# A delta-rule recurrence that takes keys times state from the values before one product with the inverse

## The chip, the cores and the metric

The kernel runs on one core of one Trainium2 chip. The metric is the device time of one execution in microseconds (us), as the median of several runs; a profile is taken of one further execution. The core's engines run side by side: TensorE (PE; its weight loads are shown apart as PEld), VectorE (DVE), ScalarE (ACT), GpSimd (POOL) and SyncE (SP), which issues most transfers. Each engine works through its own instructions in a fixed order, and waits on semaphores for the others.

## The reference, cut to what matters

One inference step of a two-layer hybrid encoder over 1024 prompt frames (with 16 meta tokens ahead) and 32 sample frames. Layer 0 holds eight gated-delta heads beside an S5 state-space unit; their outputs go through one output projection. Layer 1 is attention; each layer ends in a SwiGLU block. The part that concerns us is the recurrence of a delta head over chunks, in fp32:

```python
    rhs = jnp.concatenate([vc * bc[..., None], kc * (bc * jnp.exp(gc))[..., None]], axis=-1)
    sol = lax.linalg.triangular_solve(a_low + jnp.eye(CHUNK, dtype=a_low.dtype), rhs,
                                      left_side=True, lower=True)
    u, w = sol[..., :dv], sol[..., dv:]
    qk = jnp.where(causal, jnp.einsum('nbhid,nbhjd->nbhij', qc, kc) * decay, 0.0)

    def step(S, blk):
        q_, k_, u_, w_, qk_, g_ = blk
        v_new = u_ - jnp.einsum('bhcd,bhde->bhce', w_, S)
        o = (jnp.einsum('bhcd,bhde->bhce', q_ * jnp.exp(g_)[..., None], S)
             + jnp.einsum('bhij,bhje->bhie', qk_, v_new))
        g_last = g_[..., -1:]
        S = (S * jnp.exp(g_last)[..., None]
             + jnp.einsum('bhcd,bhce->bhde', k_ * jnp.exp(g_last - g_)[..., None], v_new))
        return S, o
```

With Z the inverse of the triangular matrix, u is Z times the scaled values and w is Z times the scaled keys, so that v_new = Z (values) - (Z keys) S = Z (values - keys S). The state S is a 128x128 matrix per head.

## The kernel before

Everything lies with features in partitions and tokens along the free axis. A head's tokens are cut into nine chunks: chunk 0 holds the 32 sample tokens and, from partition 64 on, the 16 meta tokens; chunks 1 to 8 hold 128 prompt tokens each. Earlier stages have written to DRAM, for each head, the keys, values and queries (`qkvd`), the transposed inverse of each chunk (`invd`, loaded as `ZT`) and the decayed scores (`qkd`). `egt` holds the decays exp(g), one column per chunk and head.

`recur(h)` (from L1148) runs for the eight heads. **Preparation:** SP loads k, v, ZT, the scores and the queries. In three blocks of four, four and one chunk, TensorE transposes the keys (L1165) and the values (L1172) into the PSUM tile `bg` (two buffers); ScalarE scales the keys by the decay into `ke` (L1168, one instruction per chunk); VectorE makes `kd` (L1169) and the scaled values `vk` (L1174). Then TensorE multiplies ke with the inverse (L1179), and ScalarE copies that, negated, to `nw` (L1180), so nw is -w. kd, vk and nw are slots of the tile `bw` (six buffers).

**The chunk loop** (from L1192), in one PSUM bank of `rca` for even heads and `rcb` for odd ones: inverse times values (L1195) plus nw times the state S (L1199; L1197 in chunk 0, with the sample state) make the new values, which VectorE copies out as `vn` (L1201). TensorE multiplies kd with vn (L1213; L1205 and L1209 in chunk 0), VectorE makes the new state `Sa` or `Sb` (L1214; L1206, L1211). Scores times vn (L1216) and queries times the old state (L1220; L1218) make the output, copied by ScalarE (L1221, L1223). **Head end:** norms, a GpSimd scaling of all outputs (L1232), nine transposes (L1237), the product with the gate and a store to `mixd`.

Two other kinds of work stand between these steps on TensorE. The S5 unit's gated product (`s5.glu`) multiplies gh and gl with gwh and gwl: 144 products, lines L72 to L74 into `pm`. The output projection (`out_part`) does the same with rh, rl and wh, wl; its first part reads S5's output back from `mixd` into `rraw` (L1258), one of four tiles at a time, which ScalarE and VectorE split (L37, L38); 168 of its products stand in one stretch, between steps of heads 3 and 4, 60 after the last head. They are called fillers below. An fp32 product of 128 columns is two MATMUL records in the trace; the fillers are one each.

What sets the order: the kernel is written head after head, and `tile.TileContext` with `schedule_with_timeline_sim=True` (L2057) orders each engine's instructions ahead of the run, by the planner's own model of times, by dependences and by free buffers. On the chip the order of an engine is fixed.

Of the kernel before, what the change touches and what calls it, by code (L numbers as in the profile page):

```python
# [773 lines left out]
def even_layer(cx, ctx, I, O):  # L774
# [13 lines left out]
    with ExitStack() as es:  # L788
# [34 lines left out]
        with ExitStack() as esA:  # L823
# [98 lines left out]
            v.tensor_copy(stats.rearrange("p c q -> p (c q)"), pt[:, :360])  # L922
            egt = pool.tile([128, 9, 8], F32, name="egt")
            sc.activation(egt, stats[:, :, 32:40], AF.Exp)


            sm_all = pool.tile([128, 8, 8, 9], F32, name="gsm")
# [220 lines left out]
        def recur(h):  # L1148
            sm, egl = smalls[h]
            nk, nq, rk, rq, Pm, kds = (sm[:, i] for i in (0, 1, 2, 3, 4, 6))  # L1150
            P = "ab"[h % 2]
            k, vv = bslot("bk", 2), bslot("bk", 2)
            ZT, qk, qe = (bslot("bl", 6) for i in range(3))
            nc.sync.dma_start(k[:, :TG], qkvd[8 + h])
            nc.sync.dma_start(vv[:, :TG], qkvd[16 + h])
            nc.sync.dma_start(ZT, invd[h])
            nc.sync.dma_start(qk, qkd[h])
            nc.sync.dma_start(qe[:, :TG], qkvd[h])
            Zv, qv = c3(ZT), c3(qk)
            ke = bslot("ke", 1)  # L1160
            kd, vk = bslot("bw", 6), bslot("bw", 6)
            for a, b in BK:
                p = gpt()
                for c in range(a, b):
                    nc.tensor.transpose(p[:, (c - a) * 128:(c - a + 1) * 128], k[:, C0[c]:C0[c] + 128], cx.ident)  # L1165
                pv = p[:, :(b - a) * 128].rearrange("p (c i) -> p c i", i=128)
                for c in range(a, b):
                    sc.activation(c3(ke)[:, c], pv[:, c - a], AF.Copy, scale=egt[:, c, h:h + 1])  # L1168
                v.tensor_mul(c3(kd)[:, a:b], pv, kds[:, a:b].unsqueeze(2).to_broadcast([128, b - a, 128]))  # L1169
                p = gpt()  # L1170
                for c in range(a, b):
                    nc.tensor.transpose(p[:, (c - a) * 128:(c - a + 1) * 128], vv[:, C0[c]:C0[c] + 128], cx.ident)  # L1172
                pv = p[:, :(b - a) * 128].rearrange("p (c i) -> p c i", i=128)
                v.tensor_mul(c3(vk)[:, a:b], pv, nk[:, a:b].unsqueeze(2).to_broadcast([128, b - a, 128]))  # L1174
            nw = bslot("bw", 6)
            for a, b in BK:
                p = gpt()
                for c in range(a, b):
                    nc.tensor.matmul(p[:, (c - a) * 128:(c - a + 1) * 128], c3(ke)[:, c], Zv[:, c], start=True, stop=True)  # L1179
                sc.activation(c3(nw)[:, a:b].rearrange("p c i -> p (c i)"), p[:, :(b - a) * 128], AF.Copy, scale=-1.0)  # L1180
            g.memset(c3(nw)[:, 0, 32:128], 0.0)
            q0 = bp.tile([128, 128], F32, name="q0" + P)
            g.memset(q0[:, 32:], 0.0)
            g.tensor_copy(q0[:, :32], qe[:, :32])

            o = vk
            ov = c3(o)
            ss = bp.tile([128, 9], F32, name="oss" + P)
            S = None
            Ss = bp.tile([128, 128], F32, name="Ss", bufs=2)  # L1190
            nc.sync.dma_start(Ss, I['sdelta'][h])
            for c in range(9):  # L1192
                bank = rct(P)
                p = bank[:, 0:128]
                nc.tensor.matmul(p, Zv[:, c], c3(vk)[:, c], start=True, stop=False)  # L1195
                if c == 0:
                    nc.tensor.matmul(p, c3(nw)[:, 0], Ss, start=False, stop=True)  # L1197
                else:
                    nc.tensor.matmul(p, c3(nw)[:, c], S, start=False, stop=True)  # L1199
                vn = bp.tile([128, 128], F32, name="vn" + P, bufs=2)  # L1200
                v.tensor_scalar_mul(vn, p, Pm[:, c:c + 1])  # L1201
                p2 = bank[:, 128:256]
                Sn = bp.tile([128, 128], F32, name="S" + P, bufs=3)
                if c == 0:
                    nc.tensor.matmul(p2, c3(kd)[0:32, 0], vn[0:32], start=True, stop=True)  # L1205
                    v.scalar_tensor_tensor(Sn, Ss, egl[:, 9:10], p2, op0=OP.mult, op1=OP.add)  # L1206
                    g.dma_start(O['delta'][1, h], Sn)
                    p2 = bank[:, 384:512]
                    nc.tensor.matmul(p2, c3(kd)[64:80, 0], vn[64:80], start=True, stop=True)  # L1209
                    Sn = bp.tile([128, 128], F32, name="S" + P, bufs=3)  # L1210
                    v.tensor_copy(Sn, p2)  # L1211
                else:
                    nc.tensor.matmul(p2, c3(kd)[:, c], vn, start=True, stop=True)  # L1213
                    v.scalar_tensor_tensor(Sn, S, egl[:, c:c + 1], p2, op0=OP.mult, op1=OP.add)  # L1214
                p3 = bank[:, 256:384]
                nc.tensor.matmul(p3, qv[:, c], vn, start=True, stop=False)  # L1216
                if c == 0:
                    nc.tensor.matmul(p3, q0, Ss, start=False, stop=True)  # L1218
                else:
                    nc.tensor.matmul(p3, qe[:, C0[c]:C0[c] + 128], S, start=False, stop=True)  # L1220
                sc.activation(ov[:, c], p3, AF.Copy)  # L1221
                jk = bp.tile([128, 128], F32, name="jk" + P)
                sc.activation(jk, ov[:, c], AF.Square, accum_out=ss[:, c:c + 1])  # L1223
                S = Sn
            g.dma_start(O['delta'][0, h], S)
            t = sm[:, 7]
            v.tensor_mul(t, rq, rq)
            v.tensor_mul(t, t, ss)
            sc.activation(t, t, AF.Sqrt, scale=1.0 / (128.0 * 128.0), bias=cx.eps)
            v.reciprocal(t, t)  # L1230
            v.scalar_tensor_tensor(t, t, 128.0 ** -0.5, rq, op0=OP.mult, op1=OP.mult)
            g.tensor_mul(ov, ov, t.unsqueeze(2).to_broadcast([128, 9, 128]))  # L1232
            mx = bslot("mx", 1)
            for a, b in BK:
                p = rct(P)
                for c in range(a, b):
                    nc.tensor.transpose(p[:, (c - a) * 128:(c - a + 1) * 128], ov[:, c], cx.ident)  # L1237
                if a == 0:
                    rg = ((0, 32, 0), (64, 80, 32), (128, 512, 48))
                else:  # L1240
                    rg = ((0, (b - a) * 128, a * 128 - 80),)
                for x0, x1, t0 in rg:
                    n = x1 - x0
                    sc.activation(mx[:, t0:t0 + n], p[:, x0:x1], AF.Copy, scale=og[:, 0:1])
            z = xp.tile([128, T], F32, name="zr")
            nc.sync.dma_start(z, zd[h])
            g.tensor_mul(mx[:, :T], mx[:, :T], z)
            sc.dma_start(mixd[h], mx[:, :T])
# [826 lines left out]
```

## Time and profile before

| | us |
|---|---|
| median of three runs | 3353.06 |
| lowest and highest | 3349.21, 3353.29 |
| profiled execution | 3346.38 |
| its span | 3344.6 |

The profile is of the one profiled execution; its times count from the start of the span. 1.8 us of that execution lie outside the span. The mean granted TensorE clock was 0.971 of full speed. A group of a view names line, engine, operation, output and input tile; "idle before" is the time that the engine stood still just ahead of an instruction, and the arrow names what ended it. The stage around the change runs from 708 to 937 us.

### The profile page before, as it was taken

The page shows a single profiled execution, that of the slowest core. Times are in us where ns is not written, and L with a number is a line of the kernel's source. Part 1 is how long each engine was busy: PE and PEld are TensorE (multiplying, and loading weights), DVE is VectorE, ACT ScalarE, POOL GpSimd, SP SyncE. Part 2 cuts the span into 40 slices and gives each one's busy share as a digit, 9 for nine tenths or more (in the row PEclk, how much of TensorE's full clock was granted, in tenths as well). Part 3 has the DMA queues.
Part 4 walks back from the last instruction along what each step waited for, and adds up shares of the span by engine and source line. Part 5 has one row for each costly group of instructions (what it writes and reads, how often), then busy time and mean ns, then how long its engine had stood idle before and what let it go on. Part 6 is the DMA issues. An engine that isn't in the chain of part 4 may idle for free. (4 is left out here: it accounts for less than half of the span.)

```text
span 3344.6 us, 54676 instructions
## 1 busy us (share of the span) xinstructions
PE 3171.3 (95%) x21673; PEld 3042.8 (91%) x21673; DVE 1925.0 (58%) x3654; ACT 1190.3 (36%) x2219; POOL 1004.1 (30%) x1021
## 2 busy tenths in 40 slices
PE   7998999989999999999999999988998999999997
PEld 6998998888989999999999998876888999999996
DVE  8666548945437655556346226656767655556434
ACT  5543222135434322223123115555655322223112
POOL 2144664522200555540003002222210555551003
PEclk9999999999999999999999999997998999999998
DMA  3354323356432222226123455544415222226211
GB/s 111 130 170 156 119 89 108 93 187 253 156 128 78 83 78 78 78 85 229 49 60 131 150 142 143 158 143 123 134 66 182 79 80 80 78 77 217 74 46 67
DMA packets 159785, 391.87 MB, mean 117 GB/s; under 512 B 41037, under 2 KB 70497, under 8 KB 159529
## 3 DMA queue, kind: packets, MB, share of 16 engines
q1 hardware_dynamic: 134920, 319.49, 30.1%
q10 hardware_dynamic: 16704, 44.33, 3.6%
q0 software_dynamic: 7904, 24.56, 2.2%
q8 instruction: 171, 2.80, 0.3%
q14 instruction: 86, 0.70, 0.1%
HBM read 267.09 MB, written 121.20 MB: 116 GB/s over the span
## 5 line engine op out<-in xcount | busy, mean ns | idle before, releaser
L72 PE MATMUL pm<-mv,wh 128*128 128x352 f32 (+2 forms) x2272 | 750.6, 331 | 20.1 <-DVE pre L940 9.0
L74 PE MATMUL pm<-mv,wl 128*128 128x352 f32 (+2 forms) x2272 | 747.6, 330 | 0.5 <-DVE wl L38 0.5
L73 PE MATMUL pm<-mv,wh 128*128 128x352 f32 (+2 forms) x2272 | 747.5, 329 | 0.0
L72 PEld LDWEIGHTS pm<-mv,wh 128*128 128x128 f32 (+1 forms) x2272 | 428.8, 189 | 30.8 <-issue 8.6
L73 PEld LDWEIGHTS pm<-mv,wh 128*128 128x128 f32 (+1 forms) x2272 | 428.4, 189 | 3.9 <-issue 0.9
L74 PEld LDWEIGHTS pm<-mv,wl 128*128 128x128 f32 (+1 forms) x2272 | 428.5, 189 | 3.7 <-DVE wl L38 0.8
L37 ACT ACTIVATE wh<-wraw 128x512 fp32r<-128x512 f32 (+4 forms) x182 | 148.8, 818 | 664.0 <-PE pm L73 560.8
L255 PE MATMUL pq<-mv,wl 128*128 128x268 f32 x2112 | 294.5, 290 | 9.1 <-DVE xslot L265 4.2
L255 PE MATMUL pq<-mv,wh 128*128 128x268 f32 x2112 | 288.9, 287 | 3.7 <-DVE xslot L262 1.9
L255 PEld LDWEIGHTS pq<-mv,wl 128*128 128x128 f32 x2112 | 277.5, 192 | 9.8 <-ACT mv L37 4.4
L255 PEld LDWEIGHTS pq<-mv,wh 128*128 128x128 f32 x2112 | 272.2, 188 | 4.6 <-ACT wh L37 4.5
L104 POOL TENSOR_TENSOR acc<-acc,sq 128x360 f32<-128x360 f32 (+3 forms) x35 | 35.5, 1014 | 512.1 <-ACT sq L103 511.6
L342 DVE TENSOR_TENSOR xslot<-xslot,pm 128x360 f32<-128x360 f32 x144 | 74.8, 525 | 168.3 <-PE pm L74 168.2
L236 POOL TENSOR_TENSOR sab<-wraw 128x512 f32<-128x512 f32 x20 | 26.0, 1300 | 459.8 <-DMA wraw<-in_w_dram 373.3
L38 DVE TENSOR_TENSOR wl<-wraw,wh 128x512 fp32r<-128x512 f32 (+4 forms) x144 | 134.6, 935 | 47.2 <-ACT wh L37 45.7
L947 DVE SCALAR_TENSOR_TENSOR cy<-pre,convw,cy 128x1104 f32<-128x1104 f32 x72 | 114.0, 1583 | 16.1 <-ACT cy L945 15.2
L309 POOL TENSOR_TENSOR xslot<-xslot,r 128x1072 f32<-128x1072 f32 x44 | 120.9, 2770 | 0.1
L255 PE MATMUL pq<-us,wl 128*128 128x268 f32 x858 | 119.2, 287 | 0.0
L255 PE MATMUL pq<-us,wh 128*128 128x268 f32 x858 | 118.6, 286 | 0.0
L38 DVE TENSOR_TENSOR wh<-sab,wh 128x512 fp32r<-128x512 f32 x88 | 75.6, 861 | 68.1 <-ACT wh L37 68.1
L255 PEld LDWEIGHTS pq<-us,wl 128*128 128x128 f32 x858 | 111.6, 189 | 0.0
L255 PEld LDWEIGHTS pq<-us,wh 128*128 128x128 f32 x858 | 111.0, 188 | 0.0
(773 smaller groups left out, 7062.8 us busy)
## 6 DMA issues: line engine op xcount, KB each, us to landing
ud<-xslot SPq DMA_DIRECT2D x44, 536.0 KB
sab<-ud SPq DMA_DIRECT2D x44, 536.0 KB
wraw<-in_w_dram SPq DMA_DIRECT2D x44, 512.0 KB
xraw<-in_w_dram SPq DMA_DIRECT2D x44, 512.0 KB
wraw<-in_wie_dram SPq DMA_DIRECT2D x36, 512.0 KB
qkvd<-cy ACTq DMA_DIRECT2D x24, 552.0 KB
wraw<-in_wio_dram SPq DMA_DIRECT2D x24, 512.0 KB
kq<-qkvd SPq DMA_DIRECT2D x16, 552.0 KB
```

The lines of the kernel that those rows point to most:

```text
L37: nc.scalar.activation(h, src, AF.Copy)
L38: (eng or nc.vector).tensor_sub(l, src, f(h))
L72: nc.tensor.matmul(ps, a, h[:, c0:c1], start=start and k == 0, stop=False)
L73: nc.tensor.matmul(ps, a, l[:, c0:c1], start=False, stop=False)
L74: nc.tensor.matmul(ps, b, h[:, c0:c1], start=False, stop=stop and k == kt - 1)
L104: (eng or nc.gpsimd).tensor_add(acc[:, c0:c1], acc[:, c0:c1], s)
L236: eng.tensor_add(S1, A21, A22)
L255: nc.tensor.matmul(p[:, 512 * j:512 * j + HC], op[:, wo + 128 * k:wo + 128 * k + 128], B[nm][k][:, xo + HC * j:xo + HC * j + HC], start=ne ...
L309: g.tensor_mul(o, o, r)
L342: nc.vector.tensor_add(X[m][:, c0:c1], X[m][:, c0:c1], p)
L947: v.scalar_tensor_tensor(y[:, :TG], pre[:, j:j + TG], convw[:, i, j:j + 1], y[:, :TG], op0=OP.mult, op1=OP.add)
```

## The change

The product of keys and inverse, its scaling and its copy are taken out. In each chunk, the untransposed keys are multiplied with the state (L1188 of the new kernel), VectorE multiplies that with the decay, now negated once on GpSimd, and adds the values (`u`, L1189, in the place of vk); one product with the inverse (L1191) and the copy L1193 give vn. From there on it is as before under new numbers: L1197 to L1206 make the state, L1208, L1210 and L1212 the output, L1229 transposes at the head's end. Transposes of keys and values are L1165 and L1170. The keys are read through the whole loop: they have three buffers of their own, the values two, and `bw` four.

```diff
             egt = pool.tile([128, 9, 8], F32, name="egt")
             sc.activation(egt, stats[:, :, 32:40], AF.Exp)
+            g.tensor_scalar_mul(egt, egt, -1.0)
...
-            k, vv = bslot("bk", 2), bslot("bk", 2)
+            k, vv = bslot("bk", 3), bslot("bv", 2)
...
-            ke = bslot("ke", 1)
-            kd, vk = bslot("bw", 6), bslot("bw", 6)
+            kd, vk = bslot("bw", 4), bslot("bw", 4)
...
-                for c in range(a, b):
-                    sc.activation(c3(ke)[:, c], pv[:, c - a], AF.Copy, scale=egt[:, c, h:h + 1])
...
-            nw = bslot("bw", 6)
-            for a, b in BK:
-                p = gpt()
-                for c in range(a, b):
-                    nc.tensor.matmul(p[:, (c - a) * 128:(c - a + 1) * 128], c3(ke)[:, c], Zv[:, c], start=True, stop=True)
-                sc.activation(c3(nw)[:, a:b].rearrange("p c i -> p (c i)"), p[:, :(b - a) * 128], AF.Copy, scale=-1.0)
-            g.memset(c3(nw)[:, 0, 32:128], 0.0)
...
                 bank = rct(P)
+
+                n = 128 if c else 32
+                p, u = bank[:n, 384:512], c3(vk)[:n, c]
+                nc.tensor.matmul(p, k[:, C0[c]:C0[c] + n], S if c else Ss, start=True, stop=True)
+                v.scalar_tensor_tensor(u, p, egt[:n, c, h:h + 1], u, op0=OP.mult, op1=OP.add)
                 p = bank[:, 0:128]
-                nc.tensor.matmul(p, Zv[:, c], c3(vk)[:, c], start=True, stop=False)
-                if c == 0:
-                    nc.tensor.matmul(p, c3(nw)[:, 0], Ss, start=False, stop=True)
-                else:
-                    nc.tensor.matmul(p, c3(nw)[:, c], S, start=False, stop=True)
+                nc.tensor.matmul(p, Zv[:, c], c3(vk)[:, c], start=True, stop=True)
```

Outside the stage the orders of the engines differ by a few swaps. Inside it, TensorE's order before, from head 0's first transposes on: its steps stand after all its transposes and the products of L1179, and head 1 begins much later.

```order
L1165 MATMUL bg<-ident,bk 128x128 x4
L1172 MATMUL bg<-ident,bk 128x128 x4
L1165 MATMUL bg<-ident,bk 128x128 x4
L1172 MATMUL bg<-ident,bk 128x128 x4
L1195 MATMUL rca<-bw,bl 128x128 x2
L1165 MATMUL bg<-ident,bk 128x128
L1172 MATMUL bg<-ident,bk 128x128
L1179 MATMUL bg<-bl,ke 128x128 x9
L1197 MATMUL rca<-Ss,bw 128x128
L1205 MATMUL rca<-vna,bw 128x128
L1209 MATMUL rca<-vna,bw 128x128
L1216 MATMUL rca<-vna,bl 128x128
```

TensorE after, at the same place, when the transposes of heads 0 and 1 are through (rca is head 0, rcb head 1):

```order
L1191 MATMUL rca<-bw,bl 128x128
L1191 MATMUL rcb<-bw,bl 128x128
L1205 MATMUL rca<-vna,bw 128x128
L1205 MATMUL rcb<-vnb,bw 128x128
L1208 MATMUL rca<-vna,bl 128x128
L1212 MATMUL rca<-Sa,bl 128x128
L1188 MATMUL rca<-Sa,bk 128x128
L1208 MATMUL rcb<-vnb,bl 128x128
L1212 MATMUL rcb<-Sb,bl 128x128
L1188 MATMUL rcb<-Sb,bk 128x128
```

The two heads go in lockstep: each step of head 0 is followed by the same step of head 1, ahead of the first filler.

TensorE before, near the end of the stage, where head 7 (rcb) runs alone:

```order
L1216 MATMUL rcb<-vnb,bl 128x128
L1220 MATMUL rcb<-Sb,bl 128x128
L1199 MATMUL rcb<-Sb,bw 128x128
L1195 MATMUL rcb<-bw,bl 128x128
L1213 MATMUL rcb<-vnb,bw 128x128
L1216 MATMUL rcb<-vnb,bl 128x128
```

TensorE after, at the same place:

```order
L1208 MATMUL rcb<-vnb,bl 128x128
L1212 MATMUL rcb<-Sb,bl 128x128
L1188 MATMUL rcb<-Sb,bk 128x128
L1191 MATMUL rcb<-bw,bl 128x128
L1205 MATMUL rcb<-vnb,bw 128x128
L1208 MATMUL rcb<-vnb,bl 128x128
```

The number of products in a chunk is the same; the inverse's product (L1191) reads what VectorE makes of L1188, where L1195 read the values alone.

## Rows read from the trace of the kernel before

**Rows 1.** The page, part 1: busy us (share of the span) x instructions.

```profile
PE 3171.3 (95%) x21673; PEld 3042.8 (91%) x21673; DVE 1925.0 (58%) x3654; ACT 1190.3 (36%) x2219; POOL 1004.1 (30%) x1021
```

**Rows 2.** Windows: length, busy of each engine (instructions), granted clock, DMA share, GB/s.

```profile
708.00:763.00 55.00, 48.48 (x303) 45.71 (x303) 26.84 (x45) 32.42 (x73) 7.92 (x18) 0.91 0.44 157
763.00:828.00 65.00, 58.22 (x428) 51.42 (x427) 34.78 (x89) 38.69 (x138) 18.27 (x20) 1.00 0.81 303
828.00:869.00 41.00, 41.00 (x289) 40.57 (x290) 18.95 (x45) 13.68 (x46) 5.55 (x6) 1.00 0.36 121
869.00:937.00 68.00, 58.88 (x419) 51.07 (x417) 28.90 (x88) 34.12 (x139) 21.39 (x21) 0.98 0.44 148
```

**Rows 3.** TensorE's timeline, head 7 alone: start, length, operation, idle before, releaser.

```profile
928.00 0.49 PE L1216 MATMUL rcb<-vnb,bl 128*128 128x128 f32 x2 [0.44 <-DVE Sb L1214]
...
928.54 0.39 PE L1199 MATMUL rcb<-Sb,bw 128*128 128x128 f32 x2
929.38 0.49 PE L1213 MATMUL rcb<-vnb,bw 128*128 128x128 f32 x2 [0.45 <-DVE vnb L1201]
930.30 0.49 PE L1216 MATMUL rcb<-vnb,bl 128*128 128x128 f32 x2 [0.44 <-DVE Sb L1214]
```

**Rows 4.** Groups by line and shape, 690 to 945: busy us, mean ns, idle before.

```profile
L1168 ACT ACTIVATE ke<-bg,egt 128x128 f32<-128x128 f32 x72 | 21.3, 369 | 14.6 <-PE bg L1165 14.5
...
L1179 PE MATMUL bg<-bl,ke 128*128 128x128 f32 x144 | 19.7, 278 | 2.6 <-ACT bw L1180 2.1 <-DVE bw L1174 0.4
...
L1214 DVE SCALAR_TENSOR_TENSOR Sb<-Sb,egl,rcb 128x128 f32<-128x128 f32 x32 | 11.1, 346 | 16.0 <-PE rcb L1213 15.3
```

**Rows 5.** TensorE's timeline around eight products of keys and inverse.

```profile
881.65 1.95 PE L1179 MATMUL bg<-bl,ke 128*128 128x128 f32 x16
883.44 0.39 PE L1216 MATMUL rcb<-vnb,bl 128*128 128x128 f32 x2
```

**Rows 6.** TensorE's timeline in stretch I: transposes, first chunks, first and last fillers.

```profile
708.31 0.60 PE L1165 MATMUL bg<-ident,bk 128*128 128x128 f32 x4
...
711.86 1.11 PE L1165 MATMUL bg<-ident,bk 128*128 128x128 f32 x4 [2.51 <-DVE bw L1169]
...
720.80 0.40 PE L1197 MATMUL rca<-Ss,bw 128*128 128x128 f32 x2
...
724.79 0.42 PE L1199 MATMUL rca<-Sa,bw 128*128 128x128 f32 x1
...
725.93 0.65 PE L72 MATMUL pm<-gh,gwh 128*128 128x360 f32 x1
...
727.91 0.63 PE L1213 MATMUL rca<-vna,bw 128*128 128x128 f32 x2
...
761.75 0.32 PE L73 MATMUL pm<-gl,gwh 128*128 128x360 f32 x1
...
762.91 0.33 PE L74 MATMUL pm<-gh,gwl 128*128 128x360 f32 x1
```

**Rows 7.** Fourth reload on SP's queue; TensorE's first filler of III, first product after.

```profile
815.91 0.32 SPq L1258 DMA_DIRECT2D rraw<-mixd  x1
...
828.11 0.41 PE L72 MATMUL pm<-rh,wh 128*128 128x352 f32 x1
...
869.45 0.38 PE L1213 MATMUL rca<-vna,bw 128*128 128x128 f32 x2
```

**Rows 8.** TensorE's timeline: the last chunk's last product, transposes, the projection's last block.

```profile
930.63 0.39 PE L1220 MATMUL rcb<-Sb,bl 128*128 128x128 f32 x2
935.06 1.97 PE L1237 MATMUL rcb<-ident,bw 128*128 128x128 f32 x8 [4.04 <-POOL bw L1232]
...
937.32 0.65 PE L72 MATMUL pm<-rh,wh 128*128 128x360 f32 x1
```

**Rows 9.** Window of ten us with head 7 alone, columns as in rows 2.

```profile
920.00:930.00 10.00, 7.83 (x50) 6.09 (x49) 2.89 (x9) 4.25 (x17) 2.64 (x2) 1.00 0.33 109
```

## The prediction

> **What bounds the kernel now.** I read the busy shares first: TensorE is busy 95% of the span, its weight loads 91%, VectorE 58%, ScalarE 36%, GpSimd 30% [rows 1]. By that view work taken off TensorE comes out of the time. But the share is a mean over the span, and the change touches one stage, 708 to 937 us, 229.0 us long. So the second view is this stage cut in four [rows 2]. In I (708 to 763) the products of the S5 unit stand between the chunk steps as filler, in III (828 to 869) those of the output projection; in II and IV there is almost nothing beside the recurrence. TensorE's busy time is 48.48 of 55 us, 58.22 of 65, 41.00 of 41 and 58.88 of 68: only III is full. Elsewhere it waits, and busy time understates by how much, since records of pipelined products overlap.
>
> The third view shows what it waits for. At the end head 7 is alone, and a chunk takes 930.30 - 928.00 = 2.30 us [rows 3]. In it the product of state and w starts at 928.54, the next one (L1213) at 929.38, after VectorE's new values: 0.84 us. L1216 follows 0.92 us later, after VectorE's new state. The 0.84 us is the price of one hop: a product, its end seen by VectorE, one VectorE instruction, the next product let go. The rest of the chunk is TensorE's own work. Two heads fill each other's hops; one chain cannot go faster than its hops.
>
> **The change, part by part.** *What goes.* The 72 products of keys and inverse (L1179, 144 records [rows 4]). A run of eight of them took 883.44 - 881.65 = 1.79 us [rows 5], 0.224 us each: 72 x 0.224 = 16.1 us of TensorE. ScalarE loses the 72 scalings of L1168, 21.3 us [rows 4], and the copies of w. Neither engine is full in I, II and IV, so what these 16.1 us are worth must come from the order: in III products taken out are time saved, elsewhere only where they stood in the chain.
>
> *What is added.* Per chunk one VectorE instruction (u, L1189), of the kind of L1214, 346 ns [rows 4]: 72 x 0.346 = 24.9 us, beside 28.90 busy of 68 in IV [rows 2], so VectorE is not full. But it is a wait as well. Before, inverse times values ran ahead, and w times S was the first of two hops. Now keys times S, then u, then the inverse, then the new values, then the state: three hops. What is queued behind each wait on TensorE is the other head's step, in strict order. The trace does not show this hop. Its lower bound is 0.346 + 0.224 = 0.57 us (the instruction and one product, no latency), its upper bound the 0.92 us of the state's hop; I take 0.85, since the row nearest to it is the 0.84 us hop through a VectorE instruction of the same size. A chunk alone then takes 2.30 + 0.85 = 3.15 us. Its five products are 1.12 us, so a pair of heads has 2.24 us of work in a cycle of 3.15: pairing no longer fills the chain.
>
> The Trainium skill ("TensorE: Matmul & The Clock Gate", section "Single matmul latency") has a single product of 128 columns at (398 + 128)/2.4 ns = 219 ns at the full clock. By it a hop would be about 0.57 us with the instruction, against 0.84 us in this trace, and stretch IV below would come out some 7 us shorter.
>
> *Edits at nothing.* The negation of 72 columns on GpSimd happens once, long before the stage, on an engine that is 30% busy [rows 1]. The key buffers (three, held through a head, since k is now read in every chunk) make the load of head n+3 wait for the end of head n, on SP's queue; it is needed a whole head (9 x 3.15 = 28 us) later. With two working slots a head instead of three, four slots still hold two heads, as six did. If that cover were gone, a load would cost as much as a late reload does in II.
>
> *Stretch I.* Before, head 0 begins its chunk 0 at 720.80, after transposes, scalings and the nine products of L1179, which waited for ScalarE; chunk 1 begins at 724.79 [rows 6]. After, TensorE's order has keys times S right behind the first transposes, and heads 0 and 1 run in lockstep from the start. Chunk 0 begins near 711.5, where the second group of transposes ran (711.86 [rows 6]), takes about the 4.0 us that it took before (724.79 - 720.80) plus one hop, and chunk 1 begins near 717. Against that, four rounds of both heads stand ahead of the first filler, while S5's activations and splits stand between the steps on ScalarE and VectorE: the hop of chunk 1 before took 727.91 - 724.79 = 3.12 us there [rows 6]. With one such hop and two of 0.9 a round is 5 us, and three rounds from 717 put the first filler at 732, where it was 725.93. Then 144 fillers at 0.166 (seven took 762.91 - 761.75 [rows 6]) are 23.9 us and four rounds of ten products at 0.224 are 9.0: 764.9, with uncovered waits 766 where it was 763. Bounds 758 (the early start kept) and 770.
>
> *Stretch II.* At 766 both heads are at chunk 7. Left until the filler of III: two and a half rounds to the end of head 0 and 1; the gap from a head's last product to its transposes, 935.06 - 930.63 = 4.43 us [rows 8]; chunk 0 of head 2 with four hops; eight more rounds of head 2, most of them alone, and three of head 3. That is some 14 rounds at 3.15, 44 us, with 7 us for gap and chunk 0: 817. But the filler also needs the fourth reload of S5's output. It was issued at 815.91 and the block began at 828.11, 12.2 us later [rows 7]; in the new order of SP it stands behind the loads that wait for head 2's end, near 811: 823. I take 822 where it was 828.1; bounds 814 and 828.
>
> *Stretch III.* 168 fillers at 0.166 are 27.9 us, and some 42 chunk products at 0.224 are 9.4: 37 us, full, where it was 869.45 - 828.11 = 41.3 [rows 7]. It ends at 859, ten us early.
>
> *Stretch IV.* No filler. TensorE's order after has six rounds of head 4, seven of head 5, five of head 6 and seven of head 7 one behind the other; what other heads do fits between. 25 x 3.15 = 78.8; less half of the first, plus the 4.43 us gap and 937.32 - 935.06 = 2.26 us of transposes [rows 8]: 84 us, where it was 67.9 (869.45 to 937.32). End 943, where it was 937.3.
>
> Sum: +3 - 9 - 4 + 16 = +6 us. The profiled run took 3346.38 us with a span of 3344.6, and would take 3352. The median of the runs shown is 6.7 above the profiled one; added to it the forecast is 3359.
>
> **The rivals.** *The clock falls (slower).* Place: the chunks that run alone, seven of head 7 and some five of head 2. TensorE waits longer in them: 1.12 us of products in 3.15 instead of in 2.30, 36% instead of 49%. For it: the transposes took 1.11 us for four after a wait of 2.51 us, against 0.60 before it [rows 6], the mark of 1.2 GHz instead of 2.4. Against it: in 920 to 930, alone and waiting, the granted clock was 1.00 [rows 9]. Price: at half clock the five products on the path cost twice, 1.1 us more a chunk, 12 chunks 13 us: 3372. It decides from the point where the waits of one chain pull the clock down at all; half of it gives 3366. The skill's same page (section "What's actually happening") calls the low clock the default and activity what lifts it; this trace agrees in the start of the stage, and not in 920 to 930.
>
> *The hop is cheap, the early start is kept (faster).* If the hop is 0.57 us, IV is 25 x 0.28 = 7 shorter and I ends 4 earlier, part of which II passes on: 3346 to 3348. The stage breaks even at a hop of about 0.61 us. For it: ScalarE's missing work and the lockstep start; against it: the hops of [rows 3].
>
> *TensorE's work decides (faster).* All 16.1 us come out, 3337. For it the 95%; against it the unfilled stretches.
>
> *The order is worse than walked (slower).* The planner's own times place a step behind one that really comes late, such as a transpose of a head's end in the middle of another's chain: +4 us at each of five head ends, 3379.
>
> **How the numbers follow.** Forecast 0.45, 3352 to 3365; clock 0.25; cheap hop 0.20; TensorE's work 0.05; worse order 0.05. A measurement tells 0.2%, 6.7 us, from no change: 3346.4 to 3359.8 is the same. The forecast's own case lies at that edge, 0.32 same and 0.13 slower; the cheap hop is 0.15 faster and 0.05 same. So faster 0.20, same 0.37, slower 0.43. The range for 8 in 10 reaches from the cheap hop to the whole clock case, 3345 to 3374.
>
> **What would show it.** Right: chunk 0 of head 0 near 711 to 713; head 7 alone at 3.1 to 3.2 us a chunk with two hops of 0.84 in it; the filler of III full and begun before 828; IV over 80 us. Wrong: a chunk under 2.9 us alone (cheap hop), a granted clock under 0.95 after 860 (clock), IV no longer than 68 us with TensorE full (its work decides), or an end of the stage past 955 with waits on head ends (order). Outside 708 to 945 the orders are alike but for a few swaps, and I count nothing there.

## The result, and the profile after

| | before | after |
|---|---|---|
| median of four runs | 3352.47 us | 3390.04 us |
| lowest and highest | 3349.21, 3353.29 | 3387.62, 3394.44 |
| profiled execution | 3346.38 us | 3387.62 us |
| its span, mean granted clock | 3344.6, 0.971 | 3385.8, 0.962 |

The ratio is 1.0113, 95% interval 1.0101 to 1.0125: slower by 38 us. The forecast of 3359 (3345 to 3374) was too low by 31 us, and the time lies outside its range.

The page, part 1, of after: busy us, share of the span, instructions.

```profile
PE 3187.8 (94%) x21529; PEld 3041.9 (90%) x21529; DVE 1945.6 (57%) x3726; ACT 1163.4 (34%) x2123; POOL 1007.9 (30%) x1014
```

Against [rows 1] TensorE has 144 records fewer and is busy for 16.5 us more. A record's length depends on the clock, so this already hints at a slower clock; the shares tell nothing else.

The stage by its four stretches, and two pieces of them, in after: window, length, busy of PE, PEld, DVE, ACT and POOL, granted clock, DMA share, GB/s.

```profile
715.00:777.00 62.00, 54.82 (x336) 49.43 (x335) 33.92 (x73) 28.41 (x67) 7.59 (x16) 0.92 0.43 165
777.00:849.00 72.00, 54.44 (x292) 42.82 (x290) 37.06 (x91) 24.02 (x78) 17.98 (x17) 0.81 0.73 266
849.00:885.00 36.00, 35.88 (x238) 35.32 (x238) 16.92 (x41) 7.92 (x26) 0.75 (x2) 1.00 0.23 70
885.00:980.00 95.00, 73.73 (x431) 58.26 (x429) 43.52 (x134) 31.72 (x130) 25.66 (x21) 0.86 0.38 131
...
810.00:820.00 10.00, 7.31 (x24) 5.54 (x25) 2.98 (x7) 2.35 (x7) 0.00 (x0) 0.50 0.14 53
...
960.00:970.00 10.00, 7.32 (x24) 5.25 (x23) 2.10 (x6) 1.75 (x8) 0.00 (x0) 0.50 0.00 0
```

By the marks of the prediction (first transposes, last S5 filler, first filler of III, first product behind it, last block) the lengths of after are 61.4, 72.6, 35.9 and 95.2 us, 265.1 together, where before has 54.8, 65.0, 41.3 and 67.9, 229.0. The stage is 36.1 us longer. III came out as forecast (37). IV holds most of the loss, 27.3 us; I and II are 6.6 and 7.6 us longer. II and IV each hold a piece at half clock, where in [rows 2] the clock is 0.98 or more.

TensorE's timeline of after with head 7 alone: start, length, operation, records, idle before and what ended it.

```profile
951.46 0.41 PE L1208 MATMUL rcb<-vnb,bl 128*128 128x128 f32 x2
...
951.93 0.39 PE L1188 MATMUL rcb<-Sb,bk 128*128 128x128 f32 x2
952.76 0.49 PE L1191 MATMUL rcb<-bw,bl 128*128 128x128 f32 x2 [0.44 <-DVE bw L1189]
953.69 0.49 PE L1205 MATMUL rcb<-vnb,bw 128*128 128x128 f32 x2 [0.44 <-DVE vnb L1193]
954.62 0.80 PE L1208 MATMUL rcb<-vnb,bl 128*128 128x128 f32 x2 [0.44 <-DVE Sb L1206]
...
959.19 0.79 PE L1208 MATMUL rcb<-vnb,bl 128*128 128x128 f32 x2 [0.44 <-DVE Sb L1206]
...
972.89 0.79 PE L1208 MATMUL rcb<-vnb,bl 128*128 128x128 f32 x2 [0.44 <-DVE Sb L1206]
```

The first chunk is the answer to [rows 3]: three waits of 0.44 us instead of two, and 954.62 - 951.46 = 3.16 us instead of 2.30. The new hop, from L1188 to L1191, is 952.76 - 951.93 = 0.83 us. From the next chunk on each product takes up to twice as long (0.80 for 0.41, the waits stay 0.44), and a chunk is 959.19 - 954.62 = 4.57 us; so it stays to the last, 972.89.

TensorE's timeline of after at the start of the stage and behind the last filler of I.

```profile
715.38 0.60 PE L1165 MATMUL bg<-ident,bk 128*128 128x128 f32 x4
...
725.10 0.38 PE L1188 MATMUL rcb<-Ss,bk 128*32 128x128 f32 x2 [2.41 <-DMA Ss<-in_sdelta_dram]
...
725.58 0.59 PE L1208 MATMUL rca<-vna,bl 128*128 128x128 f32 x2
...
728.63 1.08 PE L1165 MATMUL bg<-ident,bk 128*128 128x128 f32 x4 [0.96 <-DMA bk<-qkvd]
```

Head 0's first output product (725.58) stands behind a product of head 1 that waits for head 1's state from DRAM, and head 0's next chunk behind a transpose of head 2's keys, which waits for their load. The first filler came at 744.35, 29.0 us after the start; the forecast had 23.7, before had 17.6 [rows 6].

SP's waits of after from 715 to 850, by line and releaser: total, times, longest.

```profile
SPq L1155 <- PE rca L1188: 43.4, 1, 43.4
```

SP's issues of after around it: start, length, operation.

```profile
734.77 0.33 SPq L1182 DMA_DIRECT2D Ss<-in_sdelta_dram  x1
778.59 0.33 SPq L1155 DMA_DIRECT2D bk<-qkvd  x1
...
799.52 0.33 SPq L1250 DMA_DIRECT2D rraw<-mixd  x1
...
837.53 0.32 SPq L1250 DMA_DIRECT2D rraw<-mixd  x1
```

The load of head 3's keys holds SP's queue for 43.4 us, until head 0's last product of keys and state (L1188 at 778.17, 0.39 us long) has read the buffer that it refills. Behind it, in order, stand every load of head 3, the loads for the output projection and the four reloads of S5's output: the first at 799.52 (before: 779.92), the fourth at 837.53 (before: 815.91 [rows 7]). III's filler began 11.9 us after the fourth, as before (12.2).

### The profile page after: what moved, and what is told of

The parts are those of the page before. It is cut to its first block, busy times and chain, and to the rows that moved or that the text cites. A ratio compares the mean times of both kernels' runs of the same rounds, so it can differ in the third digit from the quotient of the medians.

```text
span 3385.8 us, 54368 instructions
## 1 busy us (share of the span) xinstructions
PE 3187.8 (94%) x21529; PEld 3041.9 (90%) x21529; DVE 1945.6 (57%) x3726; ACT 1163.4 (34%) x2123; POOL 1007.9 (30%) x1014
```

## The experiments

All stretches are measured by the same marks, from one profile each; the medians are of four runs or more, except where one run is marked. The first filler of III is the first product of rh and wh with 352 columns, as in [rows 7]. A median is not the stage plus a constant: the span less the stage is 3105 to 3126 us over these profiles, and two profiles of one kernel (the split bank in before) have 3105.1 and 3113.3.

| kernel | median us | ratio to before, 95% | I | II | III | IV | stage |
|---|---|---|---|---|---|---|---|
| before | 3352 to 3355 | 1 | 54.8 | 65.0 | 41.3 | 67.9 | 229.0 |
| after | 3390.04 | 1.0101 to 1.0125 | 61.4 | 72.6 | 35.9 | 95.2 | 265.1 |
| after again (one run) | 3389.68 | - | 59.8 | 72.4 | 35.9 | 97.6 | 265.6 |
| two hops | 3356.99 | 0.9997 to 1.0027 | 62.1 | 68.7 | 39.1 | 58.0 | 227.9 |
| before + hop | 3384.33 | 1.0068 to 1.0112 | 55.8 | 58.0 | 39.1 | 105.2 | 258.1 |
| work put back | 3390.45 | 1.0072 to 1.0134 | 57.6 | 64.0 | 40.4 | 103.5 | 265.5 |
| four hops | 3402.06 | 1.0132 to 1.0165 | 59.8 | 61.7 | 35.4 | 131.3 | 288.2 |
| clock held, head 7 | 3387.82 | 1.0082 to 1.0128 | 61.7 | 73.2 | 35.9 | 89.4 | 260.1 |
| clock held, heads 2 and 7 | 3391.57 | 1.0077 to 1.0139 | 58.8 | 73.9 | 34.5 | 99.4 | 266.6 |
| split bank, after | 3385.32 | 1.0072 to 1.0136 | 59.6 | 73.4 | 34.4 | 94.0 | 261.3 |
| split bank, clock held | 3380.39 | 1.0052 to 1.0098 | 62.1 | 69.2 | 35.0 | 97.9 | 264.2 |
| split bank, before | 3344.14 | 0.9960 to 0.9984 | 57.1 | 66.2 | 42.5 | 64.6 | 230.4 |
| four key buffers | 3380.97 | 1.0051 to 1.0091 | 50.9 | 62.1 | 35.6 | 104.0 | 252.5 |
| one value buffer | 3364.72 | 1.0017 to 1.0042 | 55.1 | 67.9 | 35.4 | 92.8 | 251.3 |
| both | 3361.95 | 1.0010 to 1.0040 | 56.5 | 66.5 | 35.4 | 96.2 | 254.6 |
| both, split bank | 3372.37 | 1.0038 to 1.0086 | 57.4 | 61.7 | 36.1 | 87.0 | 242.1 |

**Is the loss the third hop?** First the change without it. The inverse's product and the product of keys and state are put into one bank, and nothing lies between them.

```diff
-                p, u = bank[:n, 384:512], c3(vk)[:n, c]
-                nc.tensor.matmul(p, k[:, C0[c]:C0[c] + n], S if c else Ss, start=True, stop=True)
-                v.scalar_tensor_tensor(u, p, egt[:n, c, h:h + 1], u, op0=OP.mult, op1=OP.add)
                 p = bank[:, 0:128]
-                nc.tensor.matmul(p, Zv[:, c], c3(vk)[:, c], start=True, stop=True)
+                nc.tensor.matmul(p, Zv[:, c], c3(vk)[:, c], start=True, stop=False)
+                nc.tensor.matmul(p, k[:, C0[c]:C0[c] + 128], S if c else Ss, start=False, stop=True)
```

> The changed kernel without its third hop: keys times state goes straight into the same PSUM sum as inverse times values, as w times state did, and the VectorE instruction for u is gone. It leaves out the decay, the sign and the multiplication of that term with the inverse; everything else of the change stays: no product of keys and inverse, keys in three buffers, four working slots, both first heads in lockstep. If the hop is the cause (theory A), a chunk alone takes 2.3 us at full clock again, the last stretch falls from 95 to 62 to 68 us, and the time is 3330 to 3350, at or under before. If buffers, loads and the order that they bring are the cause (theory B), the late reloads and the gaps between heads stay, and the time stays over 3370.

It took 3356.99 us over ten runs, not told apart from before. A chunk of head 7 alone shows the two waits of 0.44 us of before. TensorE's timeline of this kernel, columns as above.

```profile
925.43 0.49 PE L1206 MATMUL rcb<-vnb,bl 128*128 128x128 f32 x2 [0.44 <-DVE Sb L1204]
...
927.74 0.49 PE L1206 MATMUL rcb<-vnb,bl 128*128 128x128 f32 x2 [0.44 <-DVE Sb L1204]
```

2.31 us a chunk, IV 58.0. So without the hop 33 us of the loss are gone. But the gain that I expected from 16 us less work is not there either: IV gave 9.9 us and I and II took 11.0. The order of this kernel is a new one as well, so the 33 us are not the price of the hop alone.

The counterpart is before with one hop more: the new values are copied and multiplied with the identity.

```diff
+                vh = bp.tile([128, 128], F32, name="vh" + P)
+                v.tensor_copy(vh, p)
+                p = bank[:, 384:512]
+                nc.tensor.matmul(p, cx.ident, vh, start=True, stop=True)
```

> The kernel before with a hop added in each chunk and nothing else: the new values are first copied by VectorE, go through a product with the identity, and only then to the scaled copy. The product of keys and inverse, the buffers and the loads stay as before. It adds 72 products of 0.224 us (16 us of TensorE) and 72 VectorE copies. Theory A: a chunk alone takes 3.1 to 3.3 us at full clock, 4.5 where the clock falls to a half, and the time is 3390 to 3415. Theory B: at most the 16 us of added work show, 3352 to 3368.

3384.33 us, 31 more than before, a little under what was expected. The same three waits stand in TensorE's timeline of this kernel.

```profile
957.15 0.49 PE L1220 MATMUL rcb<-vnb,bl 128*128 128x128 f32 x2 [0.44 <-DVE Sb L1218]
...
958.47 0.49 PE L1203 MATMUL rcb<-vhb,ident 128*128 128x128 f32 x2 [0.39 <-DVE vhb L1201]
959.40 0.49 PE L1217 MATMUL rcb<-vnb,bw 128*128 128x128 f32 x2 [0.45 <-DVE vnb L1205]
960.33 0.79 PE L1220 MATMUL rcb<-vnb,bl 128*128 128x128 f32 x2 [0.44 <-DVE Sb L1218]
```

A chunk is 960.33 - 957.15 = 3.18 us, as in after. All of the loss lies in IV (+37.3), none in II (-7.0): the change's buffers and its start are not in this kernel.

Next, after with its saved work put back: 72 products into a bank that nothing reads.

```diff
+            for a, b in BK:
+                p = gpt()
+                for c in range(a, b):
+                    nc.tensor.matmul(p[:, (c - a) * 128:(c - a + 1) * 128], c3(kd)[:, c], Zv[:, c], start=True, stop=True)
```

> The changed kernel with 72 products put back where the product of keys and inverse stood, of the same size (kd with the inverse), read by nobody: the 16.1 us of TensorE that the change saved are spent again, and the chain stays at three hops. If the saved work is worth its time, 3402 to 3410. If it only filled waits (theory A), at most 5 us more, 3387 to 3396, or less than the changed kernel where it keeps the clock up.

3390.45 against 3390.04: in the total the 16.1 us of TensorE work are worth nothing measurable. The order is a new one here too: III is 4.5 us longer with the work, II 8.6 shorter and IV 8.3 longer. And after with a fourth hop (the same copy and product with the identity as above, between L1191 and L1193):

> The changed kernel with one hop more in each chunk: the product with the inverse is copied by VectorE, goes through a product with the identity, and only then to the scaled copy. The chain has four hops. If the number of hops sets the stage (theory A), a chunk alone takes 4.0 us at full clock (3.16 and 0.84), two heads run at 4.0 to 4.2, and the time grows by about as much again as from two hops to three, 3412 to 3432. If the third hop cost so much only because it made TensorE wait and lose its clock, or because of the order, a fourth costs much less, 3392 to 3405.

3402.06, 12 us more than after: inside the range of the second reading, and far less than the first expected. A chunk of a pair is 4.13 us and IV grows by 36; but in this order SP has the loads for the projection ahead of the keys, the fourth reload comes at 820.16 instead of 837.53, and II is 10.9 us shorter. So the fourth hop is not shown to be cheap: its price and that of the order around it can't be read off a median alone.

**Is it the clock?** Head 7 gets four unread products a chunk in the gaps of its chain.

```diff
+                warm = c if h == 7 else 0
+                if warm:
+                    pw = gpt()
+                    for i in range(2):
+                        nc.tensor.matmul(pw[:, i * 128:(i + 1) * 128], Zv[:, c], c3(vk)[:, c], start=True, stop=True)
...
+                    if warm:
+                        for i in range(2, 4):
+                            nc.tensor.matmul(pw[:, i * 128:(i + 1) * 128], c3(kd)[:, c], vn, start=True, stop=True)
```

> The changed kernel with four products more in each chunk 1 to 8 of head 7, whose results nobody reads: two beside the product with the inverse, two beside the state's product, to stand in the waits of the chain that runs alone (0.9 us of work in a chunk of 3.16). If the low clock there comes from TensorE's waiting (theory A's second half), the granted clock stays at 1.00 to the last chunk, the rounds that took 4.57 us take 3.2 to 3.4, and the time is 6 to 9 us shorter, 3381 to 3384. If the clock falls for another reason, the rounds get longer, and the time is 3390 to 3400.

The window with head 7 alone in this kernel, columns as in the windows above, and its timeline.

```profile
950.00:960.00 10.00, 8.66 (x59) 6.97 (x58) 3.23 (x10) 2.04 (x9) 1.56 (x1) 1.00 0.35 111
```

```profile
951.53 0.49 PE L1216 MATMUL rcb<-vnb,bl 128*128 128x128 f32 x2
...
954.77 0.49 PE L1216 MATMUL rcb<-vnb,bl 128*128 128x128 f32 x2
...
958.01 0.49 PE L1216 MATMUL rcb<-vnb,bl 128*128 128x128 f32 x2
```

The clock stays at 1.00 and a chunk at 3.24 us (954.77 - 951.53). IV is 5.8 us shorter, near the 4 x 1.41 that four half-clocked chunks cost. The median is only 2 us lower, inside the spread of the runs and less than expected. With head 2 as well:

```diff
-                warm = c if h == 7 else 0
+                warm = c if h in (2, 7) else 0
```

> The changed kernel with the four unread products in the chunks of head 2 as well as of head 7. Adding them for head 7 alone took 5.8 us from the last stretch. If the clock is the whole excess in the second stretch too, another 6 to 8 us go there, the stage is 251 to 255 us instead of 265, and the time 3376 to 3383. If the second stretch waits for the reloads of the S5 output, it stays as long at full clock as at half, and the time is that of head 7 alone, 3384 to 3390.

Windows of this kernel, columns as above, and two of SP's issues: the load of head 5's keys and the fourth reload.

```profile
790.00:800.00 10.00, 8.50 (x33) 7.29 (x34) 2.22 (x7) 0.68 (x3) 3.32 (x4) 0.50 1.02 413
800.00:810.00 10.00, 8.67 (x55) 7.03 (x54) 3.15 (x9) 2.04 (x9) 0.21 (x1) 0.95 1.00 392
810.00:820.00 10.00, 9.11 (x61) 7.54 (x61) 4.06 (x10) 4.42 (x14) 0.00 (x0) 1.00 0.15 39
```

```profile
821.58 0.32 SPq L1155 DMA_DIRECT2D bk<-qkvd  x1
...
833.85 0.32 SPq L1258 DMA_DIRECT2D rraw<-mixd  x1
```

From 800 to 820 the clock is 0.95 and 1.00, where after has 0.54 and 0.50, and II is still 73.9 us. Head 2 ends earlier: the load of head 5's keys, which waits for head 2's last product with its keys, goes out at 821.58 instead of 832.17. The fourth reload still comes only at 833.85, 37.0 us after the first (after: 38.0), and III begins at 848.62. So in II the half clock of head 2 is not what sets the end; the late reloads are. In all the kernels the fourth reload follows the first by 33 to 42 us, and III begins 7 to 15 us behind it. This kernel came out no faster than after, 3391.57; its IV is 99.4 us, 10 more than with head 7 alone, and why is open.

**Is after's profile an odd one?** The same kernel in a second profile:

> The changed kernel once more, for a second profile: which parts of the stage repeat. By theory A the last stretch (95.2 us in the first profile) and the rounds alone (3.16 at full clock, 4.57 at half) come again within 2 us, while the first stretch, which waits for loads, may move by some us.

3389.68 us, and 59.8, 72.4, 35.9 and 97.6 for the stretches. I and IV move by 2 us from profile to profile, the stage by 0.5.

**Do the outputs, in the same PSUM bank, hold up the chain?** In [rows 3] L1216 waits 0.44 us for VectorE's new Sb, which it doesn't read; what it shares with L1214 is the bank that L1214 reads. L1208 of after waits in the same way. I gave the outputs a bank of their own, in after and in before, with one buffer of each.

```diff
-            return ps.tile([128, 512], F32, name="rc" + p, bufs=2)
+            return ps.tile([128, 512], F32, name="rc" + p, bufs=1)
...
-                p3 = bank[:, 256:384]
+                p3 = ps.tile([128, 512], F32, name="ro" + P, bufs=1)[:, 0:128]
```

> The changed kernel with each chunk's output products in a PSUM bank of their own (one bank for the chain and one for the output of each parity, instead of two shared ones), so that they need not wait for VectorE to read the state's product from the same bank and can run inside that hop. The chain keeps three hops. Theory A: a chunk alone falls from 3.16 to 2.6 to 2.8 us, since two products leave the path, the last stretch from 95 to 72 to 80 us, and the time is 3350 to 3372. Theory B: the chain's length is not what decides, and the time stays at 3385 to 3395.

> The kernel before with each chunk's output products in a PSUM bank of their own, as in the split of the changed kernel. Its chain has two hops. [...] If the split gains nothing, because the order or the clock gives it back as it did in the changed kernel, 3349 to 3358.

> The changed kernel with the output products in a bank of their own and four unread products more in each chunk 1 to 8 of heads 2 and 7, the two that run alone. The split alone had chunks of 2.80 us alone at full clock, but 3.76 for most of them at half clock. If the clock is what took the gain of the split, all chunks alone are 2.8 to 3.0 us, the clock stays at 0.95 or more after 780, the stage falls from 261 to 246 to 252 us, and the time is 3368 to 3378. If not, 3382 to 3392.

In after a lone chunk is 2.80 us at full clock instead of 3.16, but most of them run at half clock, at 3.76 us; 3385.32, which isn't told apart from after. With the unread products of the clock experiment in heads 2 and 7 it is 3380.39, above the 3368 to 3378 expected: in its profile the lone chunks of head 7 are 2.98 us and the clock is 0.94 from 860 to 980, but the stage is 264.2 us, no shorter than without them. So a higher clock did not bring the gain of the split into the stage; why is open. In before a lone chunk goes from 2.30 to 2.08 us, IV to 64.6, and the median was 3345.31, ratio 0.9975 (0.9959 to 0.9992). Since that is faster than both kernels, it was measured a second time:

> The kernel before with the output products in a bank of their own, timed in more rounds, because its first interval ended close to no change. If its gain is one of the chain, 3342 to 3349 again, and the last stretch 63 to 66 us instead of 67.9. If not, within 3 us of the kernel before.

3344.14 against 3355.24 on the same chip, 0.9972 (0.9960 to 0.9984). TensorE's timeline of this kernel, two chunks of head 7.

```profile
926.30 0.49 PE L1213 MATMUL rcb<-vnb,bw 128*128 128x128 f32 x2 [0.44 <-DVE vnb L1201]
926.62 0.39 PE L1216 MATMUL rob<-vnb,bl 128*128 128x128 f32 x2
...
928.38 0.49 PE L1213 MATMUL rcb<-vnb,bw 128*128 128x128 f32 x2 [0.44 <-DVE vnb L1201]
```

L1216 now follows L1213 without a wait, and a chunk is 928.38 - 926.30 = 2.08 us. Where the 7 to 11 us of the medians come from is open all the same: in both profiles IV gains 3.3 us, but I, II and III together lose 4.2 and 4.7, so the stage gains nothing.

**Is it the buffers?** The change also set new numbers of buffers: three for keys, two for values. Each was changed alone, then both, then both with the split bank. The edit of both:

```diff
-            k, vv = bslot("bk", 3), bslot("bv", 2)
+            k, vv = bslot("bk", 4), bslot("bv", 1)
```

> The changed kernel with a fourth key buffer and nothing else. In its trace SP stood 43.4 us, from 735 to 778.6, on the load of head 3's keys, which waits for head 0's last product with its keys; the loads of the residual and the reloads of the S5 output stood behind it, and the first reload went out at 799.5 instead of 779.9. If that wait is what makes the second stretch long (theory C: the life of the keys), the first reload goes out before 785, the second stretch falls from 72.6 to 56 to 64 us, the stage from 265 to 248 to 256, and the time is 3372 to 3382. If the three hops and the clock alone do it (theory A), the second stretch stays over 68 us and the time at 3385 to 3393.

> The changed kernel with one value buffer instead of two: head 1 can no longer start in lockstep with head 0, since its values are loaded when head 0's are through; the keys keep three buffers and their late load. If the lockstep start is what makes the first stretch long, the first filler comes before 735 counted from a start at 708, the first stretch falls from 61 to 54 to 57 us, and the time is 3380 to 3386. If it is the chain's length, the first stretch stays at 59 to 62.

> The changed kernel with four key buffers and one value buffer, as much memory as before: no lockstep and no wait of the queue for head 0's end. Theory C: both gains together, first stretch 54 to 57 us, second 55 to 63, stage 242 to 252, time 3365 to 3378. What then remains over the kernel before, 12 to 25 us, is the third hop. Theory A: 3385 to 3393.

> The same with the output products in a bank of their own. The chain has three hops but two products less: a chunk alone 2.8 us, of which 1.12 are work. If the buffers held the changed kernel back, this is its best form: stage 228 to 242 us, time 3345 to 3365, near the kernel before. If not, 3378 to 3390, as the split alone.

*Four key buffers alone*: 3380.97, 9 us less than after. SP's wait of 43.4 us is gone. The first and the fourth reload on SP's queue:

```profile
783.02 0.48 SPq L1250 DMA_DIRECT2D rraw<-mixd  x1
...
825.03 0.32 SPq L1250 DMA_DIRECT2D rraw<-mixd  x1
```

II is 62.1 us, 10.5 less than in after, as expected. IV is 8.8 us longer, and head 0's keys come late at the start. TensorE's timeline of this kernel:

```profile
721.66 1.08 PE L1165 MATMUL bg<-ident,bk 128*128 128x128 f32 x4 [11.02 <-DMA bk<-qkvd]
```

11.02 us of standing still lie ahead of the mark where I begins, so its I and its stage can't be compared with the others.

*One value buffer alone*: 3364.72, 25 us less than after, and 15 to 21 better than I had expected. TensorE's timeline of this kernel at the start of the stage:

```profile
710.06 0.60 PE L1165 MATMUL bg<-ident,bk 128*128 128x128 f32 x4
...
716.91 0.49 PE L1208 MATMUL rca<-vna,bl 128*128 128x128 f32 x2 [0.45 <-DVE Sa L1203]
...
731.28 0.65 PE L72 MATMUL pm<-gh,gwh 128*128 128x360 f32 x1
...
732.63 0.40 PE L1191 MATMUL rcb<-bw,bl 128*128 128x128 f32 x2
```

Head 0 has its first output product 6.85 us after the start (after: 10.20), and the first filler comes after 21.2 us instead of 29.0. Head 1's inverse product only follows at 732.63, so head 0 is ahead, where after has both heads in step. After that, two heads no longer end together, and head 2 begins while head 1 still runs. Two windows of this kernel:

```profile
800.00:810.00 10.00, 9.28 (x58) 7.37 (x56) 5.97 (x17) 3.79 (x14) 3.26 (x3) 0.95 0.70 243
810.00:820.00 10.00, 9.40 (x66) 8.14 (x65) 6.90 (x19) 5.18 (x18) 0.72 (x2) 1.00 0.70 231
```

where after has 0.54 and 0.50 and a lone head 2. SP's longest wait of a key load is 25.1 us instead of 43.4, the fourth reload comes at 820.97, III begins 12.2 us behind it, and later pairs take 3.24 us a chunk. So this edit brings the reloads forward as well, and the runs don't part that from the lost lockstep.

*Both*: 3361.95, 28 us less than after, and not told apart from one value buffer alone: the intervals overlap. SP still shows a wait of 27.6 us at a key load, put down to a product of head 1. The load goes out at 773.60, just as head 0's last product of keys and state (L1188 at 773.19, 0.39 us long) is through: it is the fifth key load, head 4's, and it waits for head 0's end as head 3's did in after. *Both with the split bank*: 3372.37, worse than without it and above the 3345 to 3365 expected, though its stage is the shortest of the three-hop kernels, 242.1 us. Their profiled executions took 3369.77 and 3370.08 us, so these two profiles don't show that loss: with the split the stage is 12.5 us shorter and the rest of the span 12.3 longer (3125.9 against 3113.6). Why is open.

## Why the prediction was wrong, step by step

By the stretches, forecast (with the start at 708.3) and measured: I 57.7 and 61.4, II 56 and 72.6, III 37 and 35.9, IV 84 and 95.2: 234.7 against 265.1. The stage is 30.4 us longer than forecast, and the median came out 31 us above its forecast. Two steps failed above all. The longer life of the keys was put at nothing, and it delayed the reloads that II waits for. And IV was summed at full clock.

- **The price of the hop held.** Forecast 0.85 us and 3.15 a lone chunk; measured 0.83 for the hop, 3.16 and 3.18 a chunk. The bound of 0.57 us, and so the cheap-hop rival, is out. The prediction's second way to 0.57 us was an estimate from the Trainium skill ("TensorE: Matmul & The Clock Gate", section "Single matmul latency"). The page gives that formula for a single bf16 product, not for an fp32 one of two records, and has no price of a hop; the traces show 0.26 us more than the estimate.
- **What goes is worth little.** That most of TensorE's 16.1 us lie where it isn't the bound was right: III, the full stretch, is 4.5 us longer with them put back, and the median only 0.4 us, inside the spread.
- **IV: the term was mis-sized, 84 for 95.2.** Four of the last cycles ran at half clock, 4 x 1.41 = 5.6 us; a paired cycle is 3.27 us (918.52 to 928.33 is three of them), not 3.15, some 2.4 us over 20 rounds; some 3 us are not placed. The clock stood among the rivals with 0.25, its mechanism right, its price at 1.1 us a chunk low. The evidence against it, a clock of 1.00 in [rows 9], was for chunks of 2.30 us and didn't carry over to chunks of 3.16.
- **II: "edits at nothing" failed.** This is the largest miss, 16.6 us. I asked when head n+3's keys are needed, and the cover held: no product of TensorE from 740 to 980 waits for a load. I didn't ask what stands behind that load on SP's queue: the four reloads, which the paragraph on II takes as what sets its end. That paragraph has the fourth behind loads that wait for head 2's end, near 811. What held it came earlier: head 3's keys waited for head 0's end, and the first reload went out 19.6 us later than before (12.5 counted from the stage's start). Four key buffers gave 10.5 us of II back. The other 6 us are not placed. Head 2's chain was also mis-sized: from its chunk 0's L1208 at 796.54 to chunk 8's at 834.55 are eight cycles in 38.0 us, where I had 8 x 3.15 = 25.2. With the clock of most of these cycles held up, II stayed as long, so as long as the reloads are late they are beside the wait. And in before with a third hop, whose fourth reload comes at 816.34, II is 58.0 us, close to the 56 forecast.
- **I: the lockstep start was read as a gain, and cost.** I had two heads from the start against a later first filler, +3 in sum. The chunk 0 of head 0 did begin early (716.34, 0.96 us after the first transposes), but strict order put the loads of heads 1 and 2 into head 0's chain (2.41 and 0.96 us), and two heads in step end close together (782.30 and 788.14) and leave head 2 alone behind them. One value buffer, which takes the lockstep away and brings the reloads forward, is worth 25 us in the median. The stage shows 14 of them: 6.3 in I, 4.7 in II, 2.4 in IV. The rest lies outside the stage, where profiles of one kernel differ by up to 8 us. That the lockstep is the cause is argued, not shown.
- **"The order is worse than walked"** had 0.05, with transposes at head ends as its mechanism. A head's end did stand in the way, but by another engine: in head 1's last chunk L1205 waits 1.66 us for its new values, because VectorE has head 0's norm ahead of them (L1222 at 786.14, which waited 1.78 us for ScalarE). The buffers, through the order that they allow, did more.
- **"Outside 708 to 945 I count nothing"** can't be told: of the 41.2 us between the two profiled spans the stage has 36.1, and the other 5.1 are within what the rest of the span moves between two profiles of one kernel (8.2 us for the split bank in before).

- **The marks that I named**: a lone chunk of 3.1 to 3.2 us, a full III and an IV over 80 us came; III's begin before 828 did not (849.41, or 842.3 counted from a start at 708.3). Of those that would show it wrong, the clock under 0.95 after 860 (0.89 from there to 980) and the stage's end past 955 (980.44, or 973.4 from that start) did.

What stays once the buffers are better is about 9 us (3361.95), so the change is slower than before in every form that was run. Taking the hop out saved 33 us and adding one to before cost 31, yet better buffers with the hop still in saved 28 of a loss of 38. These effects overlap, and their shares are not parted. Each edit also makes the planner find a new order, and no run holds the order fixed; two effects that were measured alone (9 and 25 us) gave 28 together. What other buffer numbers would do to before was not run.

## What to carry to other kernels

When an edit keeps a buffer longer, look up the load that refills it and read down its queue: what counts is not when that load is needed but what stands behind it in order. A hop through another engine costs its wait in every step of a lone chain, and then possibly the clock too; work saved on an engine in a stretch where it waits may be worth nothing. Where a planner sets the order, vary the buffer numbers one by one before judging a change: here they carried 28 of 38 us.

## What the runs showed of the hardware

In after head 7's lone chain fell from a granted clock of 1.00 to 0.50, and with it a chunk went from 3.16 to 4.57 us; before, with chunks of 2.30 us, stayed at 1.00 from 920 to 930 [rows 9]. The Trainium skill ("TensorE: Matmul & The Clock Gate", section "What's actually happening") has the throttled clock as the default, which activity releases, and the traces agree as far as four unread products a chunk kept it at 1.00. They draw no clean line: before with a hop more, at 3.18 us a chunk, was at full clock until 960.33 and then fell as well.

Outputs in a bank of their own shortened a lone chunk by 0.22 us in before (2.30 to 2.08) and by 0.36 in after (3.16 to 2.80), with the same instructions: the wait of an output product for VectorE's read of another part of its bank is gone. At half clock a chunk of after went from 4.57 to 3.76 us. Whether the chip or only the program's semaphores ask for that wait, no run tells.
